# Order edges between the linear attention's products and the projection's matmuls, in a hybrid encoder layer

## Chip, core and metric

The kernel runs on one core of one Trainium2 chip. The metric is the device time of one execution in microseconds, as the median of several runs. TensorE (PE) multiplies matrices, VectorE (DVE) and ScalarE (ACT) do the elementwise work, GpSimd (POOL) and SyncE (SP) help; weights come from HBM by DMA.

## What is computed

One layer, on 256 tokens of width 2048. `w_in` projects the normalised input to attention queries, keys and values (8 query heads, 2 key heads of 128), to queries, keys, values and gates of a gated linear attention (GLA, 4 heads with keys of 128 and values of 256), and to two low-rank decay inputs. Then come windowed attention, GLA in both directions, the output projection and a convolutional feed-forward part. Cut to what matters here:

```python
h = rms_norm(x, norm1_g)
proj = h @ w_in
q_a, k_a, v_a, q_g, k_g, v_g, gate_g, lr_f, lr_b = jnp.split(proj, offsets, axis=-1)
o_attn = window_attention(qa, ka, va, sink)          # softmax per head, with a sink logit
# GLA, per direction: g = log_sigmoid(lr @ wa2 + ba) / 16, b = cumsum(g) in chunks of 64
a = einsum(q * exp(b - b_ref), k * exp(b_ref - b))   # masked, then a @ v
x = x + concat([o_attn, o_gla]) @ w_out
x = x + conv_gated_ffn(rms_norm(x, norm2_g), w_up, conv_w, conv_b, w_down)
```

## The kernel before

All matmuls of the projections run in three parts: weights and activations are split into a rounded part (`hi`) and a rest (`lo`), and each output takes hi x hi, hi x lo and lo x hi (L259 to L261). The input projection is a loop over ten chunks of columns (`IN_CHUNKS`: kv, qa0, qa1, lk0, lk1, qg, vg0, vg1, gt0, gt1); each chunk is a loop over units of mostly two 128-row slices of the weights. A unit loads 512 KB (`raw`, 4 buffers), ScalarE copies them to `hi` (4 buffers), VectorE subtracts for `lo` (3 buffers), and TensorE issues 12 matmuls of 512 columns into two PSUM accumulators `ps[0]` and `ps[1]` (names `pvg` for vg0 and vg1, `pgt` for gt0 and gt1).

Attention and GLA are written between these units, as hooks: `plan` says ahead of which unit of which chunk a generator takes its next step. `A0` to `A7` are the attention heads (`attend`: scores `pss`, softmax in `sc`, transposes `pp`, value products `po`), `gk` and `gq` the transposes of the GLA keys and queries (`pk`, `pgq`), `M0` to `M3` the decays and blocks of the GLA heads (`mix`), `R0` to `R3` their value products (`pog`). The lines of `plan` around the place:

```python
(5, 0): "gk A4 A5", (5, 1): "A7", (5, 2): "A5 A6 gq",
(5, 4): "A7 A6", (5, 6): "A7",
(6, 0): "gq", (6, 1): "M0", (6, 2): "M0", (6, 3): "M1", (6, 4): "M0", (6, 5): "M1", (6, 6): "M2", (6, 7): "M1",
(7, 0): "M2", (7, 1): "M3", (7, 2): "M2", (7, 3): "M3", (7, 5): "M3", (7, 6): "R0", (7, 7): "R1",
```

Chunk 6 is vg0, chunk 7 vg1. So M0's first step is written between units 0 and 1 of vg0. In a step of M, `scaled` issues for each of two directions two matmuls of 384 columns with the decays (`pe`), ScalarE takes six exponentials of them into `es` (L480), VectorE multiplies these with keys and queries (L483); the third step issues eight 128-column block products (`p`, L501 and L504).

The place where something is written is not where it runs. The scheduler of the framework orders each engine's instructions by priority and by its own estimate of when their inputs are there; `high_priority(offset=1500)` puts the weights' copies and subtractions ahead. Every engine then works strictly in that order. The small products of attention and GLA share four PSUM buffers (`aux`), which are handed out in the order in which the program was written: a step of M can have one only when the attention tiles written ahead of it have had theirs. `in_order` adds an edge between two instructions of one engine that only fixes their order and waits for nothing.

Of the kernel before, what the change touches and what calls it, by code (L numbers as in the profile page):

```python
# [19 lines left out]
P = 128  # L20
T = 256
DM = 2048
NKT = DM // P
# [23 lines left out]
def in_units(ci):  # L47

    return [1] * 16 if ci == 0 else [3] * 5 + [1] if ci in (3, 4) else [2] * 8
# [11 lines left out]
def tile_hymba_layer(  # L61
# [15 lines left out]
    V, S, G, PE = nc.vector, nc.scalar, nc.gpsimd, nc.tensor  # L77
# [9 lines left out]
    def arena(shape, dt, name):  # L87
        return ar.tile(shape, dt, name=name, tag="ar")

    def work(shape, dt, name, tag="wk", bufs=None):  # L90
        return wk.tile(shape, dt, name=name, tag=tag, bufs=bufs or (4 if tag == "wk" else 2))

    def acc(name):
        return pacc.tile([P, 512], F32, name=name, tag="acc")

    def aux(name):
        return paux.tile([P, 512], F32, name=name, tag="aux")
# [4 lines left out]
    last = {}  # L102

    def weights(flat, first, cols, name):
        r = raw(f"r{name}")
        last["SP"] = nc.sync.dma_start(out=r[:, :cols], in_=flat[first : first + P * cols].rearrange("(p c) -> p c", p=P))
        hi = wp.tile([P, WCOLS], F32R, name=f"h{name}", tag="hi", bufs=4)
        lo = wp.tile([P, WCOLS], F32R, name=f"l{name}", tag="lo")
        with tc.high_priority(offset=1500):
            last["ACT"] = S.activation(hi[:, :cols], r[:, :cols], AF.Copy)  # L110
            last["DVE"] = V.tensor_tensor(lo[:, :cols], r[:, :cols], hi[:, :cols].bitcast(F32), ALU.subtract)  # L111
        return hi, lo

    def in_order(later, earlier):

        tc.add_manual_dep(
            later.ins, earlier.ins.name, mybir.DependencyInfo(mybir.DependencyClass.NoSync, mybir.DependencyReason.DATA),
            reason="order",
        )

    def after(engine, ins):

        in_order(ins, last[engine])

    def split(hi, lo, src):
        S.activation(hi, src, AF.Copy)
        V.tensor_tensor(lo, src, hi.bitcast(F32), ALU.subtract)
# [26 lines left out]
    def first_weights(kt):  # L154

        r = raw(f"ri0{kt}")
        src = wi[kt * P * 768 : (kt + 1) * P * 768].rearrange("(p c) -> p c", p=P)
        last["SP"] = nc.sync.dma_start(out=r[:, :768], in_=src)
        hi = wp.tile([P, WCOLS], F32R, name=f"hi0{kt}", tag="hi", bufs=4)
        lo = wp.tile([P, WCOLS], F32R, name=f"li0{kt}", tag="lo")  # L160
        w, x, g = r[:, :512], r[:, 512:768], g1[:, kt : kt + 1]
        xh, xl = hh[kt // 8][:, kt % 8], hl[kt // 8][:, kt % 8]
        with tc.high_priority(offset=1500):
            if kt == 0:
                V.tensor_scalar(xh, x, g, None, op0=ALU.mult)
            else:
                S.activation(xh, x, AF.Copy, scale=g)
            last["ACT"] = S.activation(hi[:, :512], w, AF.Copy)
            V.tensor_tensor(lo[:, :512], w, hi[:, :512].bitcast(F32), ALU.subtract)
            last["DVE"] = V.scalar_tensor_tensor(out=xl, in0=x, scalar=g, in1=xh.bitcast(F32), op0=ALU.mult, op1=ALU.subtract)  # L170
        return hi, lo
# [20 lines left out]
    def load_rows(c):  # L192
        if c % 2 == 0:
            xrows.append(arena([P, 2, 1024], F32, f"xq{c}"))
        after("SP", nc.sync.dma_start(out=xrows[c // 2][:, c % 2], in_=xr[c]))

    def token_square(c):

        for t in range(2):
            junk = work([P, 512], BF16, "junkx")  # L200
            after("ACT", S.activation(
                junk, xrows[c // 2][:, c % 2, t * 512 : t * 512 + 512], AF.Square, accum_out=ssq1[:, t, c : c + 1]
            ))
# [10 lines left out]
    def load_consts():  # L214
        after("SP", nc.sync.dma_start(out=prm_sb, in_=prm))
# [21 lines left out]
    def run_hooks(ci, u):  # L237
        for fn, args in hooks.get((ci, u), ()):
            fn(*args)

    def project(ci):
        name, _, width = IN_CHUNKS[ci]
        ps = [acc(f"p{name}{t}")[:, :width] for t in range(2)]
        kt = 0
        for u, per in enumerate(in_units(ci)):
            run_hooks(ci, u)
            if ci == 0:
                hi, lo = first_weights(kt)
                in_first[0] += P * 768
            else:  # L250
                hi, lo = weights(wi, in_first[0], per * width, f"i{name}{u}")
                in_first[0] += P * per * width
            for k in range(per):
                a, o = kt // 8, kt % 8
                wh, wl = hi[:, k * width : (k + 1) * width], lo[:, k * width : (k + 1) * width]
                for t in range(2):
                    xh = hh[a][:, o, t * P : t * P + P]
                    xl = hl[a][:, o, t * P : t * P + P]
                    PE.matmul(ps[t], xh, wh, start=(kt == 0), stop=False)  # L259
                    PE.matmul(ps[t], xh, wl, start=False, stop=False)  # L260
                    PE.matmul(ps[t], xl, wh, start=False, stop=(kt == NKT - 1))  # L261
                kt += 1
        return ps

# [205 lines left out]
    def scaled(h, t, es):  # L470
        for d in range(2):
            pe = aux(f"pe{h}{d}{t}")
            for j, src in enumerate((gh, gl)):
                PE.matmul(
                    pe[:, :384], src[:, t, d * 512 + h * P : d * 512 + h * P + P], dec_sb[:, 2 * d + t],
                    start=(j == 0), stop=(j == 1),
                )
            for at, role, to, n, sign in PARTS[d][t]:
                e = es[:, role, t].rearrange("p a s -> p (a s)")
                S.activation(e[:, to : to + n], pe[:, at : at + n], AF.Exp, scale=sign)  # L480
        for role in range(2):
            e = es[:, role, t]
            V.tensor_tensor(e, e, gkT[:, role, h, t * P : t * P + P].unsqueeze(1).broadcast_to([P, 4, P]), ALU.mult)  # L483

    def mix(h):

        es = arena([P, 2, 2, 4, P], F32, f"es{h}")
        scaled(h, 0, es)
        yield
        scaled(h, 1, es)  # L490
        yield

        def blk(role, t, what):
            return es[:, role, t, (0, 1 + t, 2 - t, 3)[what]]

        p1 = aux(f"p1{h}")
        p2 = aux(f"p2{h}")
        for s in range(2):
            for t in range(2):
                lv = 2 if s == t else 1  # L500
                PE.matmul(p1[:, (2 * s + t) * P : (2 * s + t + 1) * P], blk(0, s, lv), blk(1, t, lv), start=True, stop=True)  # L501
        for f in range(2):
            for t in range(2):
                PE.matmul(p2[:, (2 * f + t) * P : (2 * f + t + 1) * P], blk(0, t, 3 * f), blk(1, t, 3 - 3 * f), start=True, stop=True)  # L504
        at = work([P, 4, P], F32, f"at{h}", "sc", 3)
        S.activation(at.rearrange("p a s -> p (a s)"), p1, AF.Copy)
        diag = at[:, 0::3]
        for f, c in enumerate((C_MF, C_MB)):
            V.copy_predicated(
                diag, cst_sb[:, c : c + 256].bitcast(U32).rearrange("p (a s) -> p a s", a=2),  # L510
                p2[:, 2 * f * P : (2 * f + 2) * P].rearrange("p (a s) -> p a s", a=2),
            )
        split(atr[0][:, h], atr[1][:, h], at)
# [87 lines left out]
    for (ci, u), names in plan.items():  # L601
        at(ci, u, go, *names.split())
    first_ps = project(0)
    at(1, 2, kv_raw, first_ps)
    for ci in range(1, len(IN_CHUNKS)):
        ps = project(ci)
        if ci == 1:
            at(2, 2, store, ci, ps)
        else:
            store(ci, ps)  # L610
# [6 lines left out]
    for c in range(4):  # L617
        xres = raw(f"xres{c}")
        nc.sync.dma_start(out=xres[:, :1024], in_=xr[c])
        ps = [acc(f"po{c}{t}") for t in range(2)]  # L620
        for u in range(NKT // 2):
# [4 lines left out]
            for k in range(2):  # L626
                kt = 2 * u + k
                sh, sl = (oah, oal) if kt < 8 else (ogh, ogl)
                for t in range(2):
                    a = sh[:, kt % 8, t * P : t * P + P]  # L630
                    b = sl[:, kt % 8, t * P : t * P + P]
                    wh, wl = hi[:, k * 512 : k * 512 + 512], lo[:, k * 512 : k * 512 + 512]
# [101 lines left out]
    for c in range(4):  # L734
        ps = [acc(f"pd{c}{t}") for t in range(2)]
        for u in range(NFF // 2):
# [7 lines left out]
            for k, t in order:  # L744
                kt = 2 * u + k
# [3 lines left out]
                wh, wl = hi[:, k * 512 : k * 512 + 512], lo[:, k * 512 : k * 512 + 512]  # L749
# [118 lines left out]
```

## Time and profile before

| What | Value |
|---|---|
| median of 3 runs | 1063.92 us (1063.69 to 1065.83) |
| the profiled execution | 1065.21 us, its span 1063.4 us |
| TensorE busy | 1055.9 us, 99% |
| VectorE, ScalarE busy | 703.7 us (66%), 581.7 us (55%) |
| granted TensorE clock | 1.000 in the mean |
| read from HBM | 202.25 MB, 192 GB/s over the span |

The span goes from the first to the last instruction in the trace; the execution's own time is a little longer. The rest of this document compares times with the median, and reads waits and durations in the profiled execution. Busy time of TensorE includes matmuls that overlap: the starts of neighbouring matmuls tell the pace.

### The profile page before, as it was taken

To read this page: it belongs to the slowest core of one execution; us is meant where nothing else is said; L and a number is where in the kernel's file an instruction comes from. 1 tells how busy PE (TensorE), PEld (TensorE's weight loads), DVE (VectorE), ACT (ScalarE), POOL (GpSimd) and SP (SyncE) were. 2 spreads that over 40 slices of the span, in tenths; PEclk is the share of its full clock that TensorE was granted. 3 is DMA by queue.
4 is the path that set the end of the run, shared out by engine and by line. 5 is a ranking of instruction groups with operands and counts; after the bars stand their busy time and mean duration, and the time that the engine had idled before them with its cause. 6 is when DMAs were issued, how large, how long until landed. Compare 5 with 4: busy or idle time off the path is not lost.

```text
span 1063.4 us, 13494 instructions
## 1 busy us (share of the span) xinstructions
PE 1055.9 (99%) x4892; PEld 880.4 (83%) x4892; DVE 703.7 (66%) x957; ACT 581.7 (55%) x803; POOL 15.2 (1%) x16
## 2 busy tenths in 40 slices
PE   9999999999999999999999999999999999999998
PEld 7789888888888888888888888888888888888887
DVE  6598786755555567777777777777777755444543
ACT  6745686764445455656556565656556544433342
POOL 0021000010000000000000000000000000000000
PEclk9999999999999999999999999999999999999999
DMA  8955754346656797787887887788778767676762
GB/s 257 372 166 160 224 165 137 119 138 180 198 185 223 194 251 215 216 211 226 221 216 214 213 224 219 216 211 227 219 216 214 208 194 215 194 210 193 215 196 81
DMA packets 104706, 216.76 MB, mean 204 GB/s; under 512 B 53056, under 2 KB 53568, under 8 KB 104640
## 3 DMA queue, kind: packets, MB, share of 16 engines
q1 hardware_dynamic: 57888, 204.23, 62.8%
q10 hardware_dynamic: 46752, 11.68, 7.8%
q8 instruction: 38, 0.62, 0.2%
q14 instruction: 28, 0.23, 0.1%
HBM read 202.25 MB, written 2.10 MB: 192 GB/s over the span
## 4 chain that ended last, share of the span: by engine, by line
PE 95%; DMA 3%; DVE 1%; ACT 1%; issue 0%; DVEq 0%; SPq 0%; ACTq 0%
PE pu L678 15%; PE pu L677 15%; PE pu L679 15%; PE pd L752 8%; PE pd L750 7%; PE pd L751 7%; PE po L634 2%; PE po L635 2%; PE po L633 2%; PE pgt L259 1%; PE pqa L260 1%; PE pvg L260 1%; PE pvg L261 1%; PE pgt L261 1%; PE pgt L260 1%; PE pvg L259 1%
## 5 line engine op out<-in xcount | busy, mean ns | idle before, releaser
L111 DVE TENSOR_TENSOR lu<-ru,hu 128x1024 fp32r<-128x1024 f32 x176 | 215.1, 1222 | 124.8 <-PE pu L678 68.0
L679 PE MATMUL pu<-hu,xs 128*128 128x512 f32 x704 | 274.1, 389 | 0.0
L678 PE MATMUL pu<-lu,xs 128*128 128x512 f32 x704 | 273.9, 389 | 0.0
L677 PE MATMUL pu<-hu,xs 128*128 128x512 f32 x704 | 267.2, 389 | 0.0
L110 ACT ACTIVATE hu<-ru 128x1024 fp32r<-128x1024 f32 x176 | 186.8, 1061 | 145.7 <-PE pu L679 97.7
L111 DVE TENSOR_TENSOR ld<-rd,hd 128x1024 fp32r<-128x1024 f32 x88 | 107.7, 1224 | 112.5 <-PE pd L751 103.4
L110 ACT ACTIVATE hd<-rd 128x1024 fp32r<-128x1024 f32 x88 | 93.6, 1064 | 133.6 <-PE pd L752 128.2
L677 PEld LDWEIGHTS pu<-hu,xs 128*128 128x128 f32 x704 | 132.1, 188 | 27.5
L678 PEld LDWEIGHTS pu<-lu,xs 128*128 128x128 f32 x704 | 132.1, 188 | 27.4
L679 PEld LDWEIGHTS pu<-hu,xs 128*128 128x128 f32 x704 | 132.2, 188 | 27.4
L751 PE MATMUL pd<-ld,g 128*128 128x512 f32 x352 | 136.9, 389 | 0.0
L752 PE MATMUL pd<-hd,g 128*128 128x512 f32 x352 | 136.9, 389 | 0.0
L750 PE MATMUL pd<-hd,g 128*128 128x512 f32 x352 | 136.3, 389 | 0.0
L751 PEld LDWEIGHTS pd<-ld,g 128*128 128x128 f32 x352 | 66.1, 188 | 13.8
L752 PEld LDWEIGHTS pd<-hd,g 128*128 128x128 f32 x352 | 66.1, 188 | 13.7
L750 PEld LDWEIGHTS pd<-hd,g 128*128 128x128 f32 x352 | 66.1, 188 | 13.7
L111 DVE TENSOR_TENSOR lo<-ro,ho 128x1024 fp32r<-128x1024 f32 x32 | 38.8, 1223 | 39.0 <-ACT ho L110 29.1
L715 ACT ACTIVATE c<-v,prm_sb 128x256 f32<-128x256 f32 x88 | 48.2, 595 | 22.7 <-DVE c L719 19.5
L110 ACT ACTIVATE ho<-ro 128x1024 fp32r<-128x1024 f32 x32 | 33.9, 1060 | 46.9 <-DMA ro<-in_wo_dram 26.8
L716 DVE SCALAR_TENSOR_TENSOR c<-v,prm_sb,c 128x255 f32<-128x255 f32 x88 | 40.3, 478 | 0.6 <-ACT c L715 0.6
L685 ACT ACTIVATE us<-pu,rstd 128x512 f32<-128x512 f32 x44 | 29.9, 681 | 19.6 <-PE pu L679 19.6
L719 DVE SCALAR_TENSOR_TENSOR c<-v,prm_sb,c 128x255 f32<-128x255 f32 x88 | 40.2, 477 | 0.0
(215 smaller groups left out, 1432.6 us busy)
## 6 DMA issues: line engine op xcount, KB each, us to landing
ru<-in_wu_dram SPq DMA_DIRECT2D x176, 512.0 KB, 4.3
rd<-in_wd_dram SPq DMA_DIRECT2D x88, 512.0 KB, 4.4
ro<-in_wo_dram SPq DMA_DIRECT2D x32, 512.0 KB, 3.8
riqa<-in_wi_dram SPq DMA_DIRECT2D x16, 512.0 KB, 6.2
rivg<-in_wi_dram SPq DMA_DIRECT2D x16, 512.0 KB, 4.1
rigt<-in_wi_dram SPq DMA_DIRECT2D x16, 512.0 KB, 3.6
ri<-in_wi_dram SPq DMA_DIRECT2D x16, 384.0 KB, 4.1
riqg<-in_wi_dram SPq DMA_DIRECT2D x8, 512.0 KB, 5.0
```

Of the source, the lines that this page charges most:

```text
L110: last["ACT"] = S.activation(hi[:, :cols], r[:, :cols], AF.Copy)
L111: last["DVE"] = V.tensor_tensor(lo[:, :cols], r[:, :cols], hi[:, :cols].bitcast(F32), ALU.subtract)
L260: PE.matmul(ps[t], xh, wl, start=False, stop=False)
L677: PE.matmul(ps[t], a, wh, start=(kt == 0), stop=False)
L678: PE.matmul(ps[t], a, wl, start=False, stop=False)
L679: PE.matmul(ps[t], b, wh, start=False, stop=(kt == NKT - 1))
L715: S.activation(c[:, j], v[:, j], AF.Identity, bias=cb[:, n : n + 1], scale=cw[:, 1, n : n + 1])
L716: V.scalar_tensor_tensor(out=c[:, j, 1:T], in0=v[:, j, 0 : T - 1], scalar=cw[:, 0, n : n + 1], in1=c[:, j, 1:T], op0=ALU.mult, op1=ALU.add)
L719: V.scalar_tensor_tensor(out=c[:, j, 0 : T - 1], in0=v[:, j, 1:T], scalar=cw[:, 2, n : n + 1], in1=c[:, j, 0 : T - 1], op0=ALU.mult, op1=A ...
L750: PE.matmul(ps[t], a, wh, start=(kt == 0), stop=False)
L751: PE.matmul(ps[t], a, wl, start=False, stop=False)
L752: PE.matmul(ps[t], b, wh, start=False, stop=(kt == NFF - 1))
```

## The change

A chain of order edges is laid through TensorE's program. `placed` ties an instruction behind the one that was placed last. Placed are: in each unit of the projection the first matmul into `ps[0]` and the last into `ps[1]`, each decay product (`pe`) and each block product (`p`). So these products stay between the units where they are written. The other matmuls of a unit, the attention's products and the R products are not placed. Nothing is computed differently.

```diff
--- before.py
+++ after.py
@@ -122,6 +122,12 @@
 
         in_order(ins, last[engine])
 
+    def placed(ins):
+
+        if "PE" in last:
+            in_order(ins, last["PE"])
+        last["PE"] = ins
+
     def split(hi, lo, src):
         S.activation(hi, src, AF.Copy)
         V.tensor_tensor(lo, src, hi.bitcast(F32), ALU.subtract)
@@ -256,9 +262,13 @@
                 for t in range(2):
                     xh = hh[a][:, o, t * P : t * P + P]
                     xl = hl[a][:, o, t * P : t * P + P]
-                    PE.matmul(ps[t], xh, wh, start=(kt == 0), stop=False)
+                    ins = PE.matmul(ps[t], xh, wh, start=(kt == 0), stop=False)
+                    if k == 0 and t == 0:
+                        placed(ins)
                     PE.matmul(ps[t], xh, wl, start=False, stop=False)
-                    PE.matmul(ps[t], xl, wh, start=False, stop=(kt == NKT - 1))
+                    ins = PE.matmul(ps[t], xl, wh, start=False, stop=(kt == NKT - 1))
+                    if k == per - 1 and t == 1:
+                        placed(ins)
                 kt += 1
         return ps
 
@@ -471,10 +481,10 @@
         for d in range(2):
             pe = aux(f"pe{h}{d}{t}")
             for j, src in enumerate((gh, gl)):
-                PE.matmul(
+                placed(PE.matmul(
                     pe[:, :384], src[:, t, d * 512 + h * P : d * 512 + h * P + P], dec_sb[:, 2 * d + t],
                     start=(j == 0), stop=(j == 1),
-                )
+                ))
             for at, role, to, n, sign in PARTS[d][t]:
                 e = es[:, role, t].rearrange("p a s -> p (a s)")
                 S.activation(e[:, to : to + n], pe[:, at : at + n], AF.Exp, scale=sign)
@@ -498,10 +508,14 @@
         for s in range(2):
             for t in range(2):
                 lv = 2 if s == t else 1
-                PE.matmul(p1[:, (2 * s + t) * P : (2 * s + t + 1) * P], blk(0, s, lv), blk(1, t, lv), start=True, stop=True)
+                placed(PE.matmul(
+                    p1[:, (2 * s + t) * P : (2 * s + t + 1) * P], blk(0, s, lv), blk(1, t, lv), start=True, stop=True
+                ))
         for f in range(2):
             for t in range(2):
-                PE.matmul(p2[:, (2 * f + t) * P : (2 * f + t + 1) * P], blk(0, t, 3 * f), blk(1, t, 3 - 3 * f), start=True, stop=True)
+                placed(PE.matmul(
+                    p2[:, (2 * f + t) * P : (2 * f + t + 1) * P], blk(0, t, 3 * f), blk(1, t, 3 - 3 * f), start=True, stop=True
+                ))
         at = work([P, 4, P], F32, f"at{h}", "sc", 3)
         S.activation(at.rearrange("p a s -> p (a s)"), p1, AF.Copy)
         diag = at[:, 0::3]
```

What this makes of the order shows on TensorE around M0's first decay products (`pe_1600`, `pe_1606`). Before, they stand among matmuls of vg1 (`pvg_1836`, `pvg_1837`; `hivg_2005` is its unit 5), behind the value products of head 7 (`po_1478`):

```order
L260 MATMUL pvg_1836<-livg_2006,hh_81 128x512
L132 MATMUL po_1478<-pT_1475,kvr 128x256
L133 MATMUL po_1478<-pT_1475,kvr 128x256
L131 MATMUL po_1478<-pT_1475,kvr 128x256
L132 MATMUL po_1478<-pT_1475,kvr 128x256
L133 MATMUL po_1478<-pT_1475,kvr 128x256
L474 MATMUL pe_1600<-dec_sb,gh 128x384
L474 MATMUL pe_1600<-dec_sb,gl 128x384
L474 MATMUL pe_1606<-dec_sb,gh 128x384
L474 MATMUL pe_1606<-dec_sb,gl 128x384
L261 MATMUL pvg_1836<-hivg_2005,hl_82 128x512
```

In the changed kernel TensorE goes from unit 1 of vg0 (`pvg_1568`, `hivg_1616`) to the scores of heads 4 and 5 (`pss_1180`, `pss_1226`), and behind these to the transposes of head 4 (`pp_1269`):

```order
L269 MATMUL pvg_1568<-hivg_1616,hl_80 128x512
L265 MATMUL pvg_1568<-hivg_1616,hh_79 128x512
L268 MATMUL pvg_1568<-livg_1617,hh_79 128x512
L137 MATMUL pss_1180<-kvr,qT_108 128x256
L138 MATMUL pss_1180<-kvr,qT_108 128x256
...
L139 MATMUL pss_1180<-kvr,qT_109 128x256
L139 MATMUL pss_1226<-kvr,qT_109 128x256
L389 MATMUL pp_1269<-prm_sb,sc_1181 128x128 x2
L137 MATMUL pss_1301<-kvr,qT_108 128x256
```

From there on to M0's decay products it has small products alone, 78 from the first score on, and these are the last of them (`pgq` the query transposes, `pp_1470` a half of head 7's) and the rest of unit 1:

```order
L139 MATMUL po_1478<-pT_1431,kvr 128x256
L466 MATMUL pgq_1569<-prm_sb,kv_gq 128x128 x4
L466 MATMUL pgq_1575<-prm_sb,kv_gq 128x128 x4
L389 MATMUL pp_1470<-prm_sb,sc_1382 128x128 x2
L484 MATMUL pe_1600<-dec_sb,gh 128x384
L484 MATMUL pe_1600<-dec_sb,gl 128x384
L484 MATMUL pe_1606<-dec_sb,gh 128x384
L484 MATMUL pe_1606<-dec_sb,gl 128x384
L265 MATMUL pvg_1567<-hivg_1616,hh_79 128x512
L268 MATMUL pvg_1567<-livg_1617,hh_79 128x512
L269 MATMUL pvg_1567<-hivg_1616,hl_80 128x512
```

So the attention's products of heads 4 to 7, which stood between large matmuls of vg0 and vg1, now stand in one block ahead of the rest of vg0's unit 1.

ScalarE follows. Behind the logarithm of the gates (L432) it had, before, the weights' copies (`hivg`) between the decays' copies (`gh`), the exponentials of heads 4 and 5 (`sc_1181`, `sc_1227`) and what follows:

```order
L432 ACTIVATE na<-na,ones 128x2048
L110 ACTIVATE hivg_1747<-rivg_1745 128x1024
L437 ACTIVATE gh<-mn 128x1024 x2
L110 ACTIVATE hivg_1780<-rivg_1778 128x1024
L370 ACT_TABLE_LOAD
L370 ACTIVATE m<-m,prm_sb 128x2 x2
L110 ACTIVATE hivg_1814<-rivg_1812 128x1024
L369 ACTIVATE sc_1181,m<-sc_1181,m 128x256 x2
L369 ACTIVATE sc_1227,m<-sc_1227,m 128x256 x2
L110 ACTIVATE hivg_1854<-rivg_1852 128x1024
L110 ACTIVATE hivg_1887<-rivg_1885 128x1024
L110 ACTIVATE hivg_1921<-rivg_1919 128x1024
```

and has now (line numbers are shifted by 6 or 10):

```order
L442 ACTIVATE na<-na,ones 128x2048
L380 ACT_TABLE_LOAD
L380 ACTIVATE m<-m,prm_sb 128x2 x2
L447 ACTIVATE gh<-mn 128x1024 x2
L379 ACTIVATE sc_1181,m<-sc_1181,m 128x256 x2
L379 ACTIVATE sc_1227,m<-sc_1227,m 128x256 x2
L458 ACTIVATE gkT<-pk_1336 128x512
L380 ACTIVATE m<-m,prm_sb 128x2
L379 ACTIVATE sc_1302,m<-sc_1302,m 128x256 x2
L458 ACTIVATE gkT<-pk_1342 128x512
L132 ACTIVATE pT_1274<-pp_1269 128x512
L132 ACTIVATE pT_1360<-pp_1355 128x512
```

The weights' copies have left this stretch, the table for exponentials is loaded at once, and the copy of head 4's transposed weights (`pT_1274`) stands behind head 6's exponentials (`sc_1302`) and both copies of the key transposes.

## Rows read from the trace of the kernel before

**Rows 1.** Page: busy us (share) xinstructions, and the chain by engine.

```profile
PE 1055.9 (99%) x4892; PEld 880.4 (83%) x4892; DVE 703.7 (66%) x957; ACT 581.7 (55%) x803; POOL 15.2 (1%) x16
...
PE 95%; DMA 3%; DVE 1%; ACT 1%; issue 0%; DVEq 0%; SPq 0%; ACTq 0%
```

**Rows 2.** Waits of TensorE: line, waited for: us, times, longest.

```profile
PE p L501 <- DVE es L483: 0.2, 1, 0.2
PE pgt L259 <- ACT vg L276: 0.2, 1, 0.2
```

**Rows 3.** TensorE's timeline: start, us, line, tile, shapes.

```profile
133.03 0.48 PE L261 MATMUL pvg<-hivg,hl 128*128 128x512 f32 x1
...
137.70 0.28 PE L131 MATMUL pss<-kvr,qT 128*128 128x256 f32 x1
...
138.89 0.40 PE L260 MATMUL pvg<-livg,hh 128*128 128x512 f32 x1
...
140.28 0.39 PE L259 MATMUL pvg<-hivg,hh 128*128 128x512 f32 x1
...
146.17 0.39 PE L261 MATMUL pvg<-hivg,hl 128*128 128x512 f32 x1
```

**Rows 4.** The chain, merged steps: start, us, what.

```profile
153.59 0.44 PE pp L379 x4
...
176.72 0.70 PE pe L474 x4
...
206.48 0.67 PE p L501 x6
```

**Rows 5.** VectorE's timeline, same columns as rows 3.

```profile
135.27 0.69 DVE L127 TENSOR_TENSOR qT<-ptq,qT 128x512 fp32r<-128x512 f32 x1
...
138.79 2.36 DVE L435 TENSOR_TENSOR mn<-mn,na 128x1024 f32<-128x1024 f32 x2 [0.75 <-ACT na L432]
...
141.07 0.54 DVE L363 CUSTOM_DVE_ANT_0 sc<-pss,cst_sb,prm_sb 128x256 f32<-128x256 f32 x1
...
142.93 1.22 DVE L438 TENSOR_TENSOR gl<-mn,gh 128x1024 fp32r<-128x1024 f32 x1
...
158.19 0.15 DVE L371 TENSOR_TENSOR m<-m 128x2 f32<-128x2 f32 x1
...
158.58 0.62 DVE L374 TENSOR_SCALAR sc<-sc,m 128x256 f32<-128x256 f32 x2
...
178.45 1.29 DVE L483 TENSOR_TENSOR es<-es,gkT 128x512 f32<-128x512 f32 x2 [0.37 <-ACT es L480]
```

**Rows 6.** ScalarE's timeline, same columns as rows 3.

```profile
136.75 2.01 ACT L432 ACTIVATE na<-na,ones 128x2048 f32<-128x2048 f32 x1
...
140.05 2.20 ACT L437 ACTIVATE gh<-mn 128x1024 fp32r<-128x1024 f32 x2 [0.35 <-DVE mn L435]
...
143.21 1.28 ACT L370 ACT_TABLE_LOAD   x1
...
144.51 0.48 ACT L370 ACTIVATE m<-m,prm_sb 128x2 f32<-128x2 f32 x2
...
145.85 0.49 ACT L369 ACTIVATE sc<-sc,m 128x256 f32<-128x256 f32 x1
...
154.06 0.60 ACT L126 ACTIVATE pT<-pp 128x512 fp32r<-128x512 f32 x1 [0.96 <-PE pp L379]
...
177.25 1.95 ACT L480 ACTIVATE es<-pe 128x192 f32<-128x192 f32 x9
```

**Rows 7.** Windows at the end: us, busy by engine (xcount), granted clock, DMA.

```profile
1059.00:1060.00 1.00, 0.77 (x4) 0.31 (x2) 0.33 (x2) 0.00 (x0) 0.00 (x0) 1.00 0.00 0
...
1062.00:1062.50 0.50, 0.00 (x0) 0.00 (x0) 0.00 (x0) 0.00 (x0) 0.00 (x0) 0.96 0.00 0
...
1062.50:1063.00 0.50, 0.00 (x0) 0.00 (x0) 0.00 (x0) 0.00 (x0) 0.00 (x0) 0.50 0.00 0
```

**Rows 8.** TensorE's timeline at the start.

```profile
1.05 3.82 PE L181 MATMUL warm<-ones 128*128 128x128 f32 x18 [1.05 <-DVE ones L174]
```

## Prediction

> **What bounds the kernel now.** I read the page's busy times and the chain first. TensorE is busy 1055.9 of the span's 1063.4 us and holds 95% of the chain that ended last [rows 1]. So the reader should ask of any change: does TensorE do less, or wait less? It waits 7.5 us in all. 3.6 of these lie behind its last matmul, which ends at 1059.77 [rows 7], and the waits put down to other engines inside the linear attention come to 0.2 + 0.2 us [rows 2]; what is left, 3.5 us, is the start of the program. In the thousand microseconds between, TensorE runs one matmul behind the other, because whatever small product is not ready leaves its place to a large one. That is what I looked for in the timelines of the three engines around 130 to 200 us.
>
> **What the change adds and removes.** No instruction is added or removed; the order edges cost nothing themselves. They fix, for the decay products and block products of the linear attention, between which large matmuls they stand. In the stretch it matters how late the attention runs in this kernel: the first decay products run at 176.72 [rows 4], when TensorE is in unit 5 of the second value projection, though they are written ahead of unit 1 of the first. The order of the changed kernel (shown above) puts them back there, and puts ahead of them, without a large matmul in between, all that their auxiliary PSUM buffers and transposed keys and queries wait for: the scores and transposes of heads 4 to 7, the value products of heads 4 to 6, and eight transposes each of the GLA keys and queries. These are 42 products of 256 columns, 32 transposes and 4 decay products. Their own time is unchanged: ten score products go from 137.70 to 138.89, 0.12 each [rows 3]; four transposes 0.44 and four decay products 0.70 [rows 4]; so 42 x 0.12 + 32 x 0.11 + 0.70 = 9.2 us. A large matmul takes 0.227 (26 steps from 140.28 to 146.17 [rows 3]), so in the kernel before some 130 of them lie in between, (176.7 - 137.7 - 8.5) / 0.227, and hide the softmax of four heads. In the changed one that cover is gone, and the softmax is paid.
>
> How much, worked out in the times of the trace of before, since up to here all engines have the same order. TensorE issues nine large matmuls from 133.03 [rows 3] and comes to the scores of heads 4 and 5 at 135.2; their last two products need the rest of the queries (DVE 135.27 + 0.69 [rows 5]), so they are issued by 136.6.
>
> Wait 1. ScalarE ends the logarithm of the gates at 138.7 as before. Behind it now: exponential table 1.28, two small exponentials 0.4, two copies of the decays 2.1 (2.20 with the tail of the second), four exponentials at 0.49 [rows 6]: 144.4. VectorE meanwhile does four score reductions (142.93 - 141.07 = 1.9), the two subtractions behind the logarithm (2.36) and two decay rests; the second of these, 1.2 long, starts after its copy at 142.4 and ends at 143.7. From the denominator to the first scaled half it is 158.58 + 0.31 - 158.19 = 0.7 [rows 5]. TensorE goes on at 144.6: 8.0 us idle.
>
> Wait 2. It issues two transposes of head 4, six scores of head 6, eight key transposes, two more of head 4: 2.0, to 146.6. The next product wants the copy of head 4's weights. In ScalarE's new order this stands behind a copy of keys (0.6, from 146.2), head 6's exponentials (0.2 + 1.0; their maxima, 0.93 and 0.15 on VectorE, are ready by 146.9) and a second copy (0.5), and takes 0.6 itself [rows 5, 6]: 149.2. 2.6 us idle.
>
> Wait 3. Six value products of head 4, four transposes of head 5, six scores of head 7, four transposes of head 6 and six value products of head 5 take 3.0, to 152.2. Head 7's transposes want its softmax: its reductions end at 152.2, but the maximum stands on VectorE behind the rest of head 6's weights (copy to 152.4, rest 0.6), so the exponentials run 153.2 to 154.2 and the first half is scaled at 155.0 [rows 5, 6]. 2.9 us idle.
>
> Wait 4. Two transposes, six products, eight query transposes, two transposes: 2.0, to 157.1. The two decay products wait for the copies of the query transposes: to 157.4 and 157.9. 0.4 us. The large matmuls go on at 158.3, 23.1 us after the first score; less 9.2 of work, 13.9 us are lost.
>
> Is it given back? Not on TensorE, which has no idle time left to shorten but the 0.4 us of [rows 2]; I count these as saved. Is more lost behind? The split weights of three units are ready when TensorE goes on (the pool holds three rests: 7 + 12 + 12 large matmuls, 7 us), so the next split has that time. Each later decay step puts 0.7 on a unit of 12 x 0.227 = 2.7. ScalarE needs for it six exponentials at 1.95 / 9 = 0.22 and a copy of 128x1024 (2.20 / 2 = 1.1), 2.4 in all; VectorE the two products of 1.29 and a rest of 1.2, 2.5 in all [rows 5, 6]. Both fit into 3.4 us, so I cost the later steps at nothing; if one slips by a copy or two, that is 1 to 2 us, which I keep for the range.
>
> **The clock.** Nine of these microseconds of products run between gaps of 8, 2.6 and 2.9 us, which this trace has nowhere inside. It has one such gap behind the end: TensorE idle from 1059.77, granted clock still 0.96 in the mean of 1062.0 to 1062.5, then 0.50, that is 1.2 GHz [rows 7]. So I take it that the first gap of 8 us drops the clock. What that costs is bounded from both sides. Below: nothing, if it is back with the first product. Above: every product from 144.6 on at twice its time. Then the path through them grows: 1.15 at the second wait, 2.8 more until head 7's exponentials (2.9 us of products at full rate stand on it), 2.1 in the last burst, so the large matmuls go on at 164.3 instead of 158.3, plus the climb. For the climb the nearest row is the start: 18 records of L181 take 3.82 us, 0.21 each, where six of the same size at L501 take 0.67 [rows 4, 8]; they run at half rate although the clock's column reads 1.00 there, and 1.8 us are lost until it is over. Above is thus 6.0 + 1.8 = 7.8. I take 4: the first burst (2.0 us of work, 4.0 at half rate) is as long as the start's, so some of the later ones should run at full rate, and the third gap may drop it anew. The Trainium skill (TensorE: Matmul & The Clock Gate, Part 4: PE-mode transpose) speaks against my middle: transposes, it says, do not count as TensorE's activity in the way that other matmuls do. By it the bursts here, in which 32 of 78 products are transposes, would not bring the clock back, and the sum would take the upper bound: 1063.9 + 13.5 + 7.8 = 1085.2. No row of this trace shows it either way.
>
> **The sum.** 13.9 - 0.4 + 4 = +17.5 us. The profiled execution took 1065.21 around its span of 1063.4; that is 1.3 over the median of 1063.92, so I add to the median: 1063.9 + 17.5 = 1081.4 us.
>
> **The rivals.**
>
> A, only the waits: the clock stays up or is back at once. For it: it read 1.00 in every slice until the end. Against: the tail. Then +13.5: 1077.4.
>
> B, half rate throughout: bursts of 2 to 3 us between gaps never bring it back, and the large matmuls pay the climb too: +13.5 + 7.8, and a late split of 1 to 2: 1086. For it: the start, where 3.8 us of work went by before the rate was full. Against: the burst behind the second gap is longer than that at half rate. The same page, under "HAM oscillation — how this bites in real kernels", tells of a kernel whose bursts of matmuls are shorter than the waits between them and which starts each burst throttled; by it the sum would be this rival's.
>
> C, not slower: the softmax of the four heads is ready earlier than I have it, because VectorE and ScalarE, freed of a dozen splits of weights each in this stretch, catch up. It decides where TensorE comes to the scores, 135.2: the logarithm would have to end and the exponentials be through by 136.6, but ScalarE ends it at 138.7 in an order that is unchanged until then, and 5.7 us of its own work follow [rows 6]. What it would give is the 0.4 us of [rows 2]: 1063.5. Faster than that has no source: TensorE's busy time is the same.
>
> D, the edges move nothing on the chip: excluded by the order above.
>
> **How the numbers follow.** Forecast 0.50, A 0.22, B 0.24, C 0.03, and 0.01 for something outside these. The forecast's own uncertainty is 2 us in the waits and 2 in the clock. The range leaves out C and the outer half of A and B: low is A with waits 2 us shorter, 1075; high is B with 2 us more, 1088. A measurement of this kernel tells about 0.2%, 2.1 us, from no change. Slower 0.96, same 0.03, faster 0.01.
>
> **What would show it.** In the profile after: TensorE idle about 13 to 14 us more, nearly all of it in four waits between 136 and 158 us, the longest 8 us in front of head 4's transposes and put down to L384 on VectorE, the second to the weights' copy L132 on ScalarE; the granted clock at 0.50 in a part of the stretch from 140 to 165; then TensorE without gaps, and the rest of the program shifted by a constant. Wrong would be: waits spread over the later steps of the linear attention (then the splits or the decay exponentials bind), a first wait far from 8 us (then my order of ScalarE's work is misread), or a shift without waits.

## The result

The changed kernel takes 1080.93 us in the median of four runs (1080.4 to 1081.57), beside 1063.81 us of the kernel before. The ratio is 1.0159, with a 95% interval of 1.0144 to 1.0174: 17.1 us slower, where 17.5 were forecast.

The page of the changed kernel, where it answers to [rows 1] (busy us, then the tenths by slice of 27 us):

```profile
PE 1061.3 (98%) x4892; PEld 885.5 (82%) x4892; DVE 705.5 (65%) x957; ACT 582.6 (54%) x803; POOL 15.1 (1%) x16
...
PE   9999959999999999999999999999999999999998
...
PEclk9999969999999999999999999999999999999999
```

The count of instructions is the same, and one slice alone, the sixth (135 to 162 us), has lost nearly half of TensorE's time; the granted clock is down in the same slice. Against [rows 2] two waits have appeared (us, times, longest):

```profile
PE pp L389 <- DVE sc L384: 10.7, 2, 7.9
PE po L137 <- ACT pT L132: 1.6, 1, 1.6
```

TensorE's timeline through that slice, without the large matmuls (start, us, line, tile; the idle time before an instruction in brackets):

```profile
133.68 0.28 PE L137 MATMUL pss<-kvr,qT 128*128 128x256 f32 x1
...
134.86 0.40 PE L139 MATMUL pss<-kvr,qT 128*128 128x256 f32 x2
143.17 0.66 PE L389 MATMUL pp<-prm_sb,sc 128*128 128x128 f32 x2 [7.91 <-DVE sc L384]
...
144.05 0.41 PE L139 MATMUL pss<-kvr,qT 128*128 128x256 f32 x1
144.27 0.41 PE L137 MATMUL pss<-kvr,qT 128*128 128x256 f32 x1
...
144.91 1.91 PE L457 MATMUL pk<-prm_sb,rope_kg 128*128 128x128 f32 x8
146.61 0.64 PE L389 MATMUL pp<-prm_sb,sc 128*128 128x128 f32 x2
148.84 0.58 PE L137 MATMUL po<-pT,kvr 128*128 128x256 f32 x1 [1.59 <-ACT pT L132]
...
152.41 0.63 PE L389 MATMUL pp<-prm_sb,sc 128*128 128x128 f32 x4
...
153.12 0.28 PE L139 MATMUL po<-pT,kvr 128*128 128x256 f32 x1
153.23 0.28 PE L137 MATMUL po<-pT,kvr 128*128 128x256 f32 x1
...
156.53 0.66 PE L389 MATMUL pp<-prm_sb,sc 128*128 128x128 f32 x2 [2.78 <-DVE sc L384]
...
158.27 1.54 PE L466 MATMUL pgq<-prm_sb,kv_gq 128*128 128x128 f32 x8
159.65 0.38 PE L389 MATMUL pp<-prm_sb,sc 128*128 128x128 f32 x2
...
160.95 0.39 PE L265 MATMUL pvg<-hivg,hh 128*128 128x512 f32 x1
```

Behind the first wait products of 256 columns start every 0.21 us (144.05, 144.27), from 152.4 on every 0.12 (153.12, 153.23), behind the last wait again every 0.21. From the first score to the first large matmul behind the block 27.3 us pass; less 9.2 of work, 18.1 are lost. (The spans of the two profiled executions differ by 15.7 only, mainly because the waits at the start of the program add up to 3.5 us in the one before and to 1.7 in this one.) The windows say the same of the clock (us, busy by engine, granted clock, DMA):

```profile
136.00:138.00 2.00, 0.00 (x0) 0.00 (x0) 1.98 (x7) 1.98 (x2) 0.00 (x0) 1.00 0.30 123
138.00:140.00 2.00, 0.00 (x0) 0.00 (x0) 1.77 (x4) 1.99 (x5) 0.00 (x0) 0.70 0.00 0
...
150.00:152.00 2.00, 2.00 (x12) 2.00 (x11) 1.06 (x2) 0.60 (x1) 0.00 (x0) 0.50 0.00 0
152.00:154.00 2.00, 1.75 (x13) 1.54 (x12) 0.90 (x5) 0.81 (x2) 0.00 (x0) 0.88 0.00 0
...
156.00:158.00 2.00, 1.47 (x7) 1.50 (x8) 0.62 (x2) 0.00 (x0) 0.00 (x0) 0.50 0.00 0
158.00:160.00 2.00, 2.00 (x13) 1.79 (x11) 0.00 (x0) 0.63 (x2) 0.00 (x0) 0.68 0.00 0
...
162.00:200.00 38.00, 38.00 (x201) 33.02 (x200) 26.54 (x36) 24.79 (x62) 0.00 (x0) 1.00 0.45 127
200.00:300.00 100.00, 100.00 (x485) 83.88 (x484) 55.50 (x67) 53.10 (x81) 2.78 (x4) 1.00 0.56 173
```

The clock falls within the first wait, to 0.50, comes back in the burst from 148.84 on, falls again about 156 and comes back in the last burst (0.68 from 158 to 160). From 162 to 300 TensorE has no gap.

### The profile page after: what moved, and what is told of

It is laid out like the page before. It is cut to its first block, busy times and chain, and to the rows that moved or that the text cites. A ratio compares the mean times of both kernels' runs of the same rounds, so it can differ in the third digit from the quotient of the medians.

```text
span 1079.1 us, 13496 instructions
## 1 busy us (share of the span) xinstructions
PE 1061.3 (98%) x4892; PEld 885.5 (82%) x4892; DVE 705.5 (65%) x957; ACT 582.6 (54%) x803; POOL 15.1 (1%) x16
## 4 chain that ended last, share of the span: by engine, by line
PE 94%; DMA 3%; ACT 2%; DVE 1%; issue 0%; DVEq 0%; ACTq 0%
PE pu L692 15%; PE pu L691 15%; PE pu L693 15%; PE pd L766 7%; PE pd L765 7%; PE pd L764 7%; DMA ro<-in_wo_dram 2%; PE po L648 2%; PE po L649 2%; PE po L647 2%; PE pqa L268 1%; PE pgt L265 1%; PE pgt L268 1%; PE pgt L269 1%; PE pqa L269 1%; PE pvg L269 1%
## 5 line engine op out<-in xcount | busy, mean ns | idle before, releaser
L764 PEld LDWEIGHTS pd<-hd,g 128*128 128x128 f32 x352 | 66.1, 188 | 13.7
L766 PEld LDWEIGHTS pd<-hd,g 128*128 128x128 f32 x352 | 66.1, 188 | 13.6
```

Source lines behind the costliest of these rows:

```text
L764: PE.matmul(ps[t], a, wh, start=(kt == 0), stop=False)
L766: PE.matmul(ps[t], b, wh, start=False, stop=(kt == NFF - 1))
```

## The experiments

All are edits of the changed kernel. The first four ran beside runs of the kernel before with a median of 1064.23 us, the other four beside 1064.57.

**Which ties cost.** In the first run neither the decay products nor the block products are placed; only the units' first and last matmuls are.

```diff
-                placed(PE.matmul(
+                PE.matmul(
                     pe[:, :384], src[:, t, d * 512 + h * P : d * 512 + h * P + P], dec_sb[:, 2 * d + t],
...
-                placed(PE.matmul(
+                PE.matmul(
                     p1[:, (2 * s + t) * P : (2 * s + t + 1) * P], blk(0, s, lv), blk(1, t, lv), start=True, stop=True
...
-                placed(PE.matmul(
+                PE.matmul(
                     p2[:, (2 * f + t) * P : (2 * f + t + 1) * P], blk(0, t, 3 * f), blk(1, t, 3 - 3 * f), start=True, stop=True
...
```

> Ties only among the units' first and last large matmuls; decay and block products are free, and the order puts them back among large matmuls (61 large ones stand between head 5's scores and head 4's transposes again). Theory (the cost is the softmax of heads 4 to 7, uncovered because the tied decay products stand ahead of the large matmuls): 1063 to 1065 us, no wait of TensorE above 0.5 us inside the linear attention, clock at 1.00. Rival (the chain through the units itself keeps large matmuls from filling gaps): 1068 or more, with waits in front of first matmuls of units.

Measured: 1064.19 us, ratio 1.0003 (0.9993 to 1.0012). In the trace TensorE is busy throughout from 132 to 180 us at a clock of 1.00, and its longest wait inside the linear attention, later on, is 0.4 us. The ties between units cost nothing that the interval, about 1 us either way, would show.

The second run takes the ties off the block products alone (the two lower pieces of the diff above).

> Units and decay products tied, block products free. Theory: the block of 78 small products ahead of the first decay product is unchanged, so 1080 to 1082 us, with the same waits of 8, 1.6 and 2.8 us. Rival (the ties of the block products, which want the decays' exponentials and products, cost the most): 1064 to 1072.

Measured: 1079.63 us, ratio 1.0149 (1.0134 to 1.0164), 0.4 us below the range expected, with nearly the same waits: 10.6 us in two (the longer 7.9) in front of transposes, and 1.9 in front of the value products.

The third takes them off the decay products alone (the upper piece).

> Units and block products tied, decay products free. By the order 23 large matmuls (5.2 us) stand between head 5's scores and head 4's transposes instead of none, but then one block runs to the first block products, which also want head 0's twelve decay exponentials and four products on VectorE. Theory: the first wait shrinks from 8 to about 3 us, the two behind it stay near 2 and 3, a new one of 3 to 5 us stands in front of the block products: 1075 to 1081. Rival (ties of decay products are the cause, not where the uncovered block lies): 1064 to 1068.

Measured: 1076.57 us, ratio 1.0116 (1.0101 to 1.0131), with these waits:

```profile
PE pp L389 <- DVE sc L384: 5.9, 2, 3.7
PE po L137 <- ACT pT L132: 1.6, 1, 1.6
...
PE p L511 <- DVE es L493: 0.7, 1, 0.7
PE p L511 <- ACT es L490: 0.6, 1, 0.6
```

The two costs do not add: the decay ties alone cost 15.4 us, the block ties alone 12.3, both 17.1. M0's block products are written three units behind its first decay products, so 23 large matmuls (5.2 us) lie beside the softmax, and the first wait is 3.7 in place of 7.9. The new wait in front of the block products, which I had expected at 3 to 5 us, is 1.3. What counts is where the first tied product stands: with the decay products tied, the ties of the block products add 1.7 us, which lies within the intervals of the two measurements.

**The ties, or their place.** The fourth run keeps every tie and writes the steps of M later, about where the kernel before ran them, and those of R behind them.

```diff
-        (6, 0): "gq", (6, 1): "M0", (6, 2): "M0", (6, 3): "M1", (6, 4): "M0", (6, 5): "M1", (6, 6): "M2", (6, 7): "M1",
-        (7, 0): "M2", (7, 1): "M3", (7, 2): "M2", (7, 3): "M3", (7, 5): "M3", (7, 6): "R0", (7, 7): "R1",
...
+        (6, 0): "gq",
+        (7, 3): "M0", (7, 4): "M0", (7, 5): "M1", (7, 6): "M0", (7, 7): "M1", (8, 0): "M2", (8, 1): "M1",
+        (8, 2): "M2", (8, 3): "M3", (8, 4): "M2", (8, 5): "M3", (8, 7): "M3", (9, 0): "R0 R1 R2 R3",
...
```

> All ties of the change stay, but the plan writes the linear attention's steps later, between units 3 of vg1 and 7 of gt0, about where they ran before. By the order large matmuls stand between the softmax steps again. Theory (not the ties, but the place that they tie to, costs): 1063 to 1066 us, no wait above 1 us, clock at 1.00. Rival (a tied product stalls TensorE wherever it stands, since nothing can be put in its place): 1068 to 1075, with waits in front of decay or block products.

Measured: 1063.93 us, ratio 0.9999 (0.9989 to 1.0008). Only this is left of the waits in the stretch:

```profile
PE pp L389 <- DVE sc L384: 0.3, 1, 0.3
```

So the cost is that of the place; the edges themselves cost nothing that the interval of 1 us would show. It is not faster than the kernel before either: there is no idle time to win.

**The clock.** The fifth run fills the first wait with matmuls that compute nothing.

```diff
+            for i in range(30):
+                ins = PE.matmul(pp[:, :P], ones, ones, start=True, stop=True)
+                if i == 0:
+                    in_order(ins, scores[5])
...
```

> The changed kernel, with 30 matmuls of 128x128 on a tile of ones put behind the last score of head 5, into the PSUM buffer that the transposes of head 4 fill afterwards; the scores of head 6 are tied behind head 4's first two transposes, so that the order stays. In the changed kernel TensorE waits 8.0 us there; 60 records of 0.106 each at full rate are 6.4 us and fit into the wait. They add work and no wait. Theory (the first wait drops the clock, and the half rate behind it costs 4.1 us on the path): the granted clock stays at 1.00 up to the second wait, the bursts run at 0.12 per product, waits 2 and 3 grow to about 2.6 and 2.9 us, and the time falls by 3 to 4 us to 1077 to 1078, which is the rival A of the prediction, although TensorE does 6.4 us more. Rival (the products run at half pace for another reason than the wait in front of them, or the waits of 2.6 and 2.9 us drop the clock just as well): 1080 to 1081, same as the changed kernel.

Measured: 1076.41 us (1076.26 to 1076.97), ratio 1.0111 (1.0096 to 1.0126): 4.5 us faster than the changed kernel with 6.9 us more work, 0.6 us below the range expected. TensorE's timeline, with the filling in its first row:

```profile
135.33 6.86 PE L394 MATMUL pp<-ones 128*128 128x128 f32 x60
143.32 0.44 PE L399 MATMUL pp<-prm_sb,sc 128*128 128x128 f32 x2 [1.12 <-DVE sc L389]
...
144.07 0.28 PE L139 MATMUL pss<-kvr,qT 128*128 128x256 f32 x1
144.19 0.28 PE L140 MATMUL pss<-kvr,qT 128*128 128x256 f32 x1
...
146.63 0.39 PE L138 MATMUL po<-pT,kvr 128*128 128x256 f32 x1 [1.07 <-ACT pT L133]
...
152.62 0.41 PE L399 MATMUL pp<-prm_sb,sc 128*128 128x128 f32 x2 [1.80 <-DVE sc L389]
...
156.30 0.39 PE L266 MATMUL pvg<-hivg,hh 128*128 128x512 f32 x1
```

Head 4's transposes start when they do in the changed kernel (143.32, there 143.17), so the filling costs nothing; behind them the products of 256 columns start every 0.12 again, the clock reads 1.00 in all windows from 132 to 162, and the large matmuls go on 13.0 us later instead of 17.8. (Five value products, 0.6 us, have slipped behind the first large ones.) The second and third waits did not grow as I had expected, since the order of the copies on ScalarE and VectorE shifted a little: head 4's weights are copied ahead of head 6's exponentials here. So this run shows that with the first wait filled the clock stays up and the pace stays full; its 4.5 us are not the clock's alone, because the order of the copies changed with it.

**Whose chain sets the first wait.** The sixth run replaces the logarithm, which takes two table loads out of ScalarE's program.

```diff
-        S.activation(na, na, AF.Ln, bias=ones[:, 0:1])
+        S.activation(na, na, AF.Exp, bias=ones[:, 0:1])
```

> The changed kernel with an exponential in the place of the logarithm of the gates (the gates' values are then others; left out is the logarithm alone), which takes the two table loads of 1.28 us out of ScalarE's program on either side of it. It asks whose chain sets the first wait. As the prediction told it, ScalarE alone: then both loads lie on the path, and the first wait falls from 8.0 to about 5.4 us and the time by 2.6 us or more to 1077 to 1078.5. Theory by the trace after: VectorE carries a second path of the same length (four score reductions to 137.2, the two subtractions of 2.36 us behind them, the decays' copies of 2.0 us that need these, then the exponentials), which the loads are not on: the first wait falls by 0.2 to 0.4 us only, and the time stays at 1080 to 1081.

Measured: 1080.15 us (1078.46 to 1081.52), ratio 1.0144 (1.0129 to 1.0159), and a first wait of 7.5 us. ScalarE's timeline shows where the 2.56 us went:

```profile
133.27 2.00 ACT L442 ACTIVATE na<-na,ones 128x2048 f32<-128x2048 f32 x1
135.82 0.29 ACT L380 ACTIVATE m<-m,prm_sb 128x2 f32<-128x2 f32 x1 [0.54 <-DVE m L373]
136.75 0.30 ACT L380 ACTIVATE m<-m,prm_sb 128x2 f32<-128x2 f32 x1 [0.64 <-DVE m L373]
137.88 2.19 ACT L447 ACTIVATE gh<-mn 128x1024 fp32r<-128x1024 f32 x2 [0.84 <-DVE mn L445]
```

ScalarE now waits for VectorE three times, 2.0 us in all: for the score reductions, and for the subtraction (L445) that stands behind them. VectorE has no gap there:

```profile
136.63 2.35 DVE L445 TENSOR_TENSOR mn<-mn,na 128x1024 f32<-128x1024 f32 x2
...
139.05 2.35 DVE L448 TENSOR_TENSOR gl<-mn,gh 128x1024 fp32r<-128x1024 f32 x2
141.32 0.15 DVE L381 TENSOR_TENSOR m<-m 128x2 f32<-128x2 f32 x1
```

Head 4's two exponentials are over by 141.1, but its normalisation on VectorE (L381, then L384) stands behind the second subtraction of the decays (L448) and starts when that ends. In the changed kernel the chain that ended last takes the same last steps:

```profile
140.00 2.36 DVE gl L448 x2
142.67 0.36 DVE sc L384
```

There they are set by ScalarE's logarithm, table load and copies of the decays (`gh`), here by VectorE's own reductions and subtractions. Two paths of nearly the same length end at this normalisation, and shortening one moves the end by the difference, 0.4 us. The wait shows this, not the time, whose four runs spread over 3 us.

**The gates out of the way.** The seventh run writes the second step of the gates behind the attention's last softmax.

```diff
-        (3, 3): "A3 A2", (3, 4): "A1 Q1", (3, 5): "A2 A3", (4, 0): "g", (4, 1): "g A3 Q1", (4, 2): "A4",
+        (3, 3): "A3 A2", (3, 4): "A1 Q1", (3, 5): "A2 A3", (4, 0): "g", (4, 1): "A3 Q1", (4, 2): "A4",
...
-        (5, 4): "A7 A6", (5, 6): "A7",
+        (5, 4): "A7 A6 g", (5, 6): "A7",
```

> The changed kernel with the second step of the gates (their four products, exponentials, logarithm, subtractions and decays' copies) written behind the attention's last softmax, at unit 4 of the query-gate chunk in place of unit 1 of the chunk before. Scores of heads 4 and 5 now have 20 large matmuls behind them. Theory (what is late is paid in front of the first tied product, wherever it comes from): no wait at the transposes of head 4 (under 1 us in place of 8.0), waits 2 and 3 about as before (1.5 to 3 us each), and a new one of 6 to 8 us in front of the first decay products, which now need the logarithm (2.0), its table (1.28), a subtraction and copy and rest of 1.2, 1.0 and 1.2 that have nothing beside them: 11 to 13 us of waits and 2 to 4 of clock, 1077 to 1081. Rival (the block costs by the first wait alone): with that gone, 1068 to 1071.

Measured: 1082.27 us (1080.17 to 1084.54), ratio 1.0158 (1.0141 to 1.0175); the median is 1.3 us above the range expected. The waits:

```profile
PE pe L484 <- ACT gh L447: 7.2, 1, 7.2
PE pp L389 <- DVE sc L384: 3.5, 2, 2.7
PE po L137 <- ACT pT L132: 1.9, 2, 1.2
```

The first wait is 0.8 us, and the 7 us are back in front of the first decay products, which now wait for the gates. Nothing is won by moving the work that is late from one side of the block to the other. And in the traced execution, the slowest of the four with 1084.54 us, the large matmuls pay the climb: the seven from 163.01 to 166.00 take 0.43 each in place of 0.23, 1.4 us, for which I had expected nothing. Whether the other three paid it is not shown.

**Half of the cover.** The eighth run writes M four units later, with all ties (its plan is that of the kernel shifted, so that M0 begins ahead of unit 5).

```diff
-        (6, 0): "gq", (6, 1): "M0", (6, 2): "M0", (6, 3): "M1", (6, 4): "M0", (6, 5): "M1", (6, 6): "M2", (6, 7): "M1",
...
+        (6, 0): "gq", (6, 5): "M0", (6, 6): "M0", (6, 7): "M1", (7, 0): "M0", (7, 1): "M1", (7, 2): "M2", (7, 3): "M1",
...
```

> The changed kernel with all ties kept and the steps of M and the first R written four units later (M0's first ahead of unit 5 of the first value chunk). Between the scores of heads 4 and 5 and head 4's transposes there are now 37 large matmuls, 8.4 us, and the rest of the block is unchanged. Theory (each wait is a dependent step without cover; the clock falls only after the long first one): the first wait is gone, waits 2 to 4 stay at 2.6 + 2.9 + 0.4 us or a little more, since the weights' copies stand in the same stretch, and the products run at full rate: +5.5 to +7 us, 1069 to 1071. If the gaps of 2.6 and 2.9 us drop the clock as well, up to 3 us more: 1072 to 1074. Rival (the cost is spread over the later steps of the linear attention, not over the block): these are moved with it, and the time stays at 1078 to 1081.

Measured: 1072.35 us, ratio 1.0067 (1.0048 to 1.0085), but its four runs lie apart: 1068.98 us with a mean granted clock of 1.000, and 1071.75, 1072.94 and 1073.64 with 0.997, 0.996 and 0.995. The trace is that of the first. TensorE's timeline there, the waits of the block:

```profile
147.56 0.41 PE L389 MATMUL pp<-prm_sb,sc 128*128 128x128 f32 x2 [1.88 <-DVE sc L384]
...
151.01 0.39 PE L137 MATMUL po<-pT,kvr 128*128 128x256 f32 x1 [1.25 <-ACT pT L132]
...
157.24 0.41 PE L389 MATMUL pp<-prm_sb,sc 128*128 128x128 f32 x2 [2.75 <-DVE sc L384]
...
160.43 0.39 PE L265 MATMUL pvg<-hivg,hh 128*128 128x512 f32 x1
```

The first wait did not go, as I had expected, but fell to 1.9 us: two copies of weights (1.04 and 1.05 us) have come back into ScalarE's program ahead of the exponentials, and from the first score to head 4's transposes 11.9 us pass in place of 9.5. In this execution the clock reads 1.00 in all windows from 140 to 164, through gaps of 1.9, 1.3 and 2.8 us, and the time is that expected for a clock that stays up. The other three have no trace. Their times are near the second case expected, 1072 to 1074, and their mean clock is lower, which fits a clock that these gaps dropped; where it fell is not shown. The rival, a cost spread over the later steps of the linear attention, falls here and with the fourth run.

## Why the prediction was right

**No idle time to win, the waits are new.** Right: the waits of [rows 2] were all that TensorE had inside the linear attention, and the fourth run, with every tie and no block, is level with the kernel before.

**Wait 1, 8.0 us.** From the first score to head 4's transposes 9.49 us pass, twelve scores of 0.12 and a wait of 8.1; forecast were 9.4 with 8.0 of waiting. Its size was right, and so were its last steps, VectorE's second subtraction of the decays and head 4's normalisation behind it. The cause was only half told: I had let ScalarE alone set when that subtraction starts. The sixth run shows that VectorE's own reductions and subtractions reach the same point 0.4 us earlier, so that the load that I priced at 1.28, together with the one ahead of the logarithm, is worth 0.4 there.

**Waits 2 to 4, 5.9 us at full rate.** In the changed kernel itself they read 1.6 and 2.8, with none listed in front of the decay products, because at half rate the products ahead of them take up part of the wait. So the sign that I had named, 13 to 14 us of idle time in four waits, came out as 12.3 us in three. At full rate the step from head 4's transposes to the large matmuls can be read in two traces: 13.0 us in the fifth run, 13.6 with the 0.6 that slipped, and 12.9 in the eighth (147.56 to 160.43), with nothing slipped; 158.3 - 144.6 = 13.7 were forecast. So the waits were put 0.1 to 0.8 us too high. The parts differ more, since in both traces head 4's weights are copied ahead of head 6's exponentials, which shortens the second wait.

**The clock, 4 us of a bound of 7.8.** By the steps of the upper bound: to the second wait 143.17 to 148.84, 5.67 in place of 4.6 (+1.1 of 1.15); on to head 7's transposes 7.69 in place of 5.9 (+1.8 of 2.8); from there to the large matmuls 4.42 in place of 3.2 (+1.2 of 2.1); the climb 0 of 1.8, since the large matmuls start at 0.23 (the sixth run paid 0.4 there, the seventh, whose long wait is the last, 1.4). Together 4.1, counted against the forecast's own times at full rate. The fifth run comes nearest to a measurement: 1080.93 - 1076.41 = 4.5 us, or 5.3 if each kernel is compared with the kernel before that ran beside it; the eighth run's step of 12.9 us in place of 17.8 gives 4.9. In both the order of the copies is changed as well. The reason given was right in part. The first burst, as long as the one at the start, left the clock at 0.50; the second brought it back at 152.4, the third gap dropped it anew, and the last burst brought it back once more. That the sum lies within 0.4 us is partly luck: 4 was a value between two bounds, and in the eighth run the executions of one program lay 4.7 us apart, with mean clocks from 0.995 to 1.000. Rival A was the kernel without this term, 1077.4; the fifth run came near to building it and took 1076.4. Rival B, half rate throughout, would have needed the burst of 148.84 to stay at 0.21 to its end.

The Trainium skill (TensorE: Matmul & The Clock Gate, Part 4: PE-mode transpose) says that transposes do not engage the full clock as other matmuls do, from which 1085.2 followed. The trace does not bear that out in this form: the last burst is 2 transposes, 6 value products and 10 transposes, and the eight at 158.27 take 1.38 us to the next start where the eight at 144.91 took 1.70, so the rate rose while transposes ran. How much the six value products ahead of them had to do with it is not shown.

**Later steps at nothing, no gain behind.** Right: TensorE is busy in 38.00 of the 38 us from 162 and in all of the 100 that follow, though M's steps now run there with their exponentials and products.

## What to carry to other kernels

In an engine that runs strictly in order, a small product that depends on other engines is, as here, free only as long as independent work stands between it and what it waits for. An edge that pulls it forward pulls everything along that must be done first. (That the shared PSUM buffers pull heads 4 to 7 along is read from the program and its order; no run varied their number.) So before fixing an order look up where the first such product runs, and tie it there or later. The price has two parts, the waits and the half rate behind the longer of them; in the fifth run matmuls without a purpose in the wait brought most of the second back, but the real work belongs there.

## What was not expected of the hardware

Gaps of the same length did not always have the same effect on the clock. In the eighth run's trace products behind a gap of 2.75 us went on at 0.12; in the changed kernel, behind one of 2.78, and in the seventh run, behind one of 2.75, they started every 0.21. And the clock can be won and lost again without use. In the seventh run it rose within the half-rate burst, in the last eight transposes ahead of the long wait, which end at 153.4; these windows show it (us, busy by engine, granted clock, DMA):

```profile
152.50:152.75 0.25, 0.25 (x3) 0.25 (x3) 0.25 (x2) 0.25 (x1) 0.00 (x0) 0.54 0.00 0
152.75:153.00 0.25, 0.25 (x4) 0.25 (x3) 0.25 (x1) 0.25 (x2) 0.00 (x0) 1.00 0.00 0
...
154.00:156.00 2.00, 0.00 (x0) 0.00 (x0) 0.00 (x0) 1.98 (x3) 0.00 (x0) 1.00 0.00 0
156.00:158.00 2.00, 0.00 (x0) 0.00 (x0) 0.00 (x0) 1.99 (x2) 0.00 (x0) 0.54 0.00 0
```

It stayed at 1.00 until 156, when TensorE had nothing to run, and was gone when the decay products came at 160.6, which ran at half rate (0.32 between starts of the last two, beside 0.17 in the fifth run).
